# Sixteen decay columns computed with the first head's values, and decays by one product with three row parts

## The chip, the cores and the metric

The kernel runs on one core of one Trainium2 chip. The metric is the device time of one execution in microseconds; the median of several runs is taken. In what follows PE is TensorE (the matrix engine), ACT is ScalarE, DVE is VectorE, POOL is GpSimd and SP is SyncE, whose queue issues the transfers. Lines (L286) are those of the kernel before unless it says otherwise.

## The reference, cut to what matters

A trunk of two layers on a sequence of 1024 tokens with 1024 features, float32. Layer 0 is a softmax attention with a forgetting gate, layer 1 a gated linear attention (GLA); each is followed by a SwiGLU channel mixer, and every sub-layer is normalised and modulated by a conditioning vector. The change lies in the start of the GLA:

```
proj = h @ w_in                                    # 1024 x (512 + 512 + 1024 + 1024 + 16)
q, k, v, r, a_lr = split(proj, [512, 1024, 2048, 3072])
log_alpha = log_sigmoid(a_lr @ w_a2 + b_a) / 16    # a_lr: 1024 x 16, w_a2: 16 x 512
# per head (4 heads, 128 key and 256 value channels), in chunks of 64 tokens:
b = cumsum(log_alpha within the chunk)
q_in, k_in = q * exp(b), k * exp(-b);  k_dec = k * exp(b_last - b)
A = tril(q_in @ k_in.T);  o = A @ v + q_in @ state
state = exp(b_last) * state + k_dec.T @ v
o = rms_norm(o) * g_o * silu(r)
```

So the decays of every head come from 16 columns of the projection (a_lr, columns 3072 to 3087 of w_in), multiplied by a 16 x 512 matrix.

## The kernel before

**Numbers.** Every float32 operand of a product is split in two parts, hi (rounded to the format that PE reads fast) and lo (the rest), and a product is three matmuls, hi·hi, hi·lo and lo·hi, accumulated in PSUM: `mm3`, lines L286, L287 and L288. `split` makes the two parts: a cast on ACT (L174) and a subtraction on DVE (L175). Weights come by `load_w` (L209), which loads 8 k-tiles of 128 rows by 128 columns, or 4 by 256, into one of three raw buffers, casts them in two pieces on ACT (L223) and subtracts in four pieces, three on POOL and one on DVE (L227). `Weights.next` keeps three loads ahead of their use, in the order of one list. The hi and lo parts take turns through a ring of slots, so a later load's cast waits until the matmuls that read that slot are done.

**The start of the GLA.** `h1`, the normalised input, has features on partitions and tokens along the free axis, in eight tiles of hi and lo, and is made in two token halves of 512. With it the kernel computes, for head 0:

- the values, `gv_body`: per pair of token tiles (128 tokens each) one PSUM bank with 2 x 256 columns; `proj_tok` does 24 matmuls of 256 columns per token tile (8 k-tiles, three products). Two weight loads hold k-tiles 0 to 3 (`wv_0`) and 4 to 7 (`wv_4`).
- the 16 low-rank columns, `a_body`: weights `aw` from `load_w16` in a tile padded to 128 columns, with the hi part in columns 0 to 15, the lo part in 32 to 47 and zeros elsewhere; per token half 16 matmuls of 512 columns (`aps`, L1860 and L1861). `sum16` adds the two row groups; the result is split into `aT`, hi in rows 0 to 15 and lo in rows 32 to 47, tokens along the free axis.
- the decays, `gate_z`: per head and token half two matmuls of 512 columns (`z`, L1889 and L1890), of `aT` with the hi and with the lo part of `w2t`, the second matrix in two row copies; then absolute value on ACT (L1891) and minimum on DVE (L1892).
- `gate_body`: exponential and logarithm on ACT (L1899, L1900, each with a load of a function table), subtraction, prefix scan on DVE (L1901, L1904), `dec` (L1908), and the exponentials `ei` and `t2` (L1914, L1915).
- `head_front`: the keys `gk` and queries `gqp`, each two token halves of 24 matmuls of 512 columns, multiplied by the exponentials on DVE (L1929, L1930, L1944).
- `r_proj`: the output gates `gr`, four products of 24 matmuls of 512 columns (two value halves dv, two token halves hf), with SiLU on ACT (L2042).
- `head_back`: transposes of the decayed keys (`kdt`), the products within a chunk (`at`), the states (`kv`, `S_t`), the outputs (`go`), their norm and transposes (`ogt`). `weave` mixes into it what is left of `r_proj`; the values and decays of the next head follow in the program and are drawn in where the order allows.

**Order.** The engines' instruction orders come from a list scheduler that simulates the program when it is built, bound by data dependencies, by the order in which buffers of a ring are given out, and by manual orderings (`tc.issue_after`, `behind_all`). On the chip each engine then runs its list in order. In the PSUM the rings are: `pj` with three banks (gv, aps, z, gr, gk, gqp in turn), `opr` with two (go), and one each for `at`, `kv` and `trr` (transposes).

Before, the program text for head 0 reads: values of token tiles 0 to 3; low-rank columns and decays of half 0; gates `gr` (dv 0, hf 0); values of tiles 4 and 5; low-rank columns and decays of half 1 with `gate_body`; values of tiles 6 and 7; then `head_front` and `head_back`, into which the other three gate products go. A stream of conditioning products for later sub-layers (`ada1`: transfers `ad_s` on SP, L414; pieces on DVE, L475 and L477) is spread over the whole stage.

Of the kernel before, what the change touches and what calls it, by code (L numbers as in the profile page):

```python
# [9 lines left out]
F32 = mybir.dt.float32  # L10
FR = mybir.dt.float32r
# [5 lines left out]
P = 128  # L17
# [3 lines left out]
HALF = 512  # L21
# [32 lines left out]
def trunk(ctx, tc, x, c, ada_w, ada_b, norm1_g, norm2_g, ffn_w_in, ffn_w_out,  # L54
          fox_w_in, fox_b_f, fox_w_out, gla_w_in, gla_w_a2, gla_b_a, gla_g_o,
          gla_w_out, final_g, out, dbg=None, stop=None):
    nc = tc.nc
# [3 lines left out]
    big = ctx.enter_context(tc.tile_pool(name="big", bufs=1))  # L61
    psp = ctx.enter_context(tc.tile_pool(name="psp", bufs=1, space=bass.MemoryType.PSUM))
# [95 lines left out]
    ident = cst.tile([P, P], F32, name="ident")  # L158
# [14 lines left out]
    def split(hi, lo, src):  # L173
        nc.scalar.copy(hi, src)  # L174
        nc.vector.tensor_sub(lo, src, hi.bitcast(F32))  # L175

    wr = Ring(big, names[0:3])
    ws = Ring(big, names[3:9])
# [21 lines left out]
    def leave_ffn():  # L200
        if opr_:
            ws.q = deque(opr_["sg"] + list(opr_["r"].q))
            opr_.clear()

    def load_w(src, name, ws=ws, later=False):

        kk, m = src.shape[0] // P, src.shape[1]
        raw = wr([P, kk, m], F32, name)
        nc.sync.dma_start(raw, src.rearrange("(k p) m -> p k m", p=P))  # L209
        leave_ffn()  # L210
        w = Pair(ws([P, kk, m], FR, name + "h"), ws([P, kk, m], FR, name + "l"))
        flat = lambda t: t.rearrange("p k m -> p (k m)")
        hi, lo, rw = flat(w.hi), flat(w.lo), flat(raw)
        n = kk * m

        def behind(e):
            return tc.issue_after(split_after[e]) if split_after else ExitStack()

        def parts(his=(0, 1), los=(0, 1, 2, 3)):
            for i in his:  # L220
                cs = slice(i * n // 2, (i + 1) * n // 2)
                with behind("A"):
                    nc.scalar.copy(hi[:, cs], rw[:, cs])  # L223
            for i in los:
                cs = slice(i * n // 4, (i + 1) * n // 4)
                with behind("G" if i < 3 else "D"):
                    (nc.gpsimd if i < 3 else nc.vector).tensor_sub(lo[:, cs], rw[:, cs], hi[:, cs].bitcast(F32))  # L227
        if later:
            return w, parts
        parts()  # L230
        return w


    split_after = {}
# [31 lines left out]
    def sum16(out, t, ps):  # L266

        nc.scalar.copy(t, ps[32:48, :])
        nc.vector.tensor_add(out, ps[0:16, :], t)

    class Weights:
# [7 lines left out]
        def next(self):  # L279
            while self.loads and len(self.got) < self.depth:  # L280
                f, *a = self.loads.popleft()
                self.got.append(f(*a))
            return self.got.popleft()

    def mm3(ps, ah, al, bh, bl, start, stop):
        nc.tensor.matmul(ps, ah, bh, start=start, stop=False)  # L286
        nc.tensor.matmul(ps, ah, bl, start=False, stop=False)  # L287
        nc.tensor.matmul(ps, al, bh, start=False, stop=stop)  # L288
# [8 lines left out]
    def proj_tok(ps, w2, hs, t):  # L297

        ts_ = psl(t)
        for k in range(8):  # L300
            w = w2[k // 4]
            mm3(ps, hs[k].hi[:, ts_], hs[k].lo[:, ts_], w.hi[:, k % 4, :], w.lo[:, k % 4, :], k == 0, k == 7)
            yield 0.33


    acc_sl, s1_sl = names[9:10], names[10:11]
# [67 lines left out]
    for t in range(6):  # L374
        nt, src = (4, rows2[0:8, :]) if t < 4 else (2, crow)
# [32 lines left out]
    def last_of(e):  # L408
        return next(i for i in reversed(nc.cur_bb.bb.instructions) if i.engine == ENG[e])
# [95 lines left out]
    ada0, ada0p, ada1 = Pace(), Pace(), Pace()  # L505
# [169 lines left out]
    sp_ins, rb_ins, root_ins = [], [], {}  # L675
# [95 lines left out]
    sr, tr, orr, pj = ps_rings(2, 3, 1, 2)  # L771
# [169 lines left out]
    Wg = gla_w_in[0]  # L941
    loads = []
# [4 lines left out]
        loads += w_loads(W, D + (p + 1) * P)  # L947
    loads += out_loads(fox_w_out[0], 0, 4) + 2 * out_loads(fox_w_out[0], 4, 4)
    loads += ffn_loads(0)
    loads += v_loads(Wg, 1024) + [(load_w16, Wg[:, 3072:3088], "aw", ws, "all")]  # L950
    for h in range(4):
        if h:
            loads += v_loads(Wg, 1024 + h * 256)
# [5 lines left out]
    feed = Weights(loads)  # L959
# [119 lines left out]
    for n, (d, hf) in enumerate(rest0):  # L1079
# [23 lines left out]
        if n in late_tr:  # L1103
            tp, i = late_tr[n]
# [682 lines left out]
    rest_of_norm, norm_end = [], []  # L1787
# [20 lines left out]
    h1 = hs1  # L1808
# [10 lines left out]
    vr = Ring(big, take(5))  # L1819
    aslot, wslot = take(2)  # L1820
# [4 lines left out]
    kdr = Ring(big, take(2))  # L1825
# [11 lines left out]
    pj, atr, kvr, opr, trr = ps_rings(3, 1, 1, 2, 1)  # L1837
# [3 lines left out]
    on_t = big.tile([P, 2, 2, 256], F32, tag=on_slot, name="on_t")  # L1841
    QS = 128 ** -0.5

    w2raw = wr([64, 512], F32, "w2raw")
    nc.sync.dma_start(w2raw[0:16, :], gla_w_a2[0])
    nc.sync.dma_start(w2raw[32:48, :], gla_w_a2[0])
    w2t = big.tile([P, 2, 512], FR, tag=wslot, name="w2t")
    aT = big.tile([P, S], FR, tag=aslot, name="aT")

    def w2_split():  # L1850
        nc.gpsimd.memset(w2t.bitcast(F32), 0.0)
        nc.gpsimd.memset(aT.bitcast(F32), 0.0)
        for r0 in (0, 32):
            split(w2t[r0:r0 + 16, 0, :], w2t[r0:r0 + 16, 1, :], w2raw[r0:r0 + 16, :])

    def a_body(aw, hf, bt):
        ps = pj([P, HALF], F32, f"aps{hf}")
        cs = hsl(hf)
        for k in range(8):
            nc.tensor.matmul(ps, aw[:, k, :], h1[k].hi[:, cs], start=k == 0, stop=False)  # L1860
            nc.tensor.matmul(ps, aw[:, k, :], h1[k].lo[:, cs], start=False, stop=k == 7)  # L1861
        a = bt[1][0:16, cs]
        sum16(a, bt[0][0:16, cs], ps)
        nc.scalar.copy(aT[0:16, cs], a)
        nc.vector.tensor_sub(aT[32:48, cs], a, aT[0:16, cs].bitcast(F32))

    def gv_body(h, wv, tp, behind=None):

        ps = pj([P, 2, 256], F32, f"gv{h}{tp}")
        for i in range(2):  # L1870
            with tc.issue_after(behind) if behind is not None and i else ExitStack():
                run(proj_tok(ps[:, i, :], wv, h1, 2 * tp + i))
        if h:
            ada1(5.1)
        v = vr([P, 2, 2, 256], FR, f"gvt{h}{tp}")
        split(v[:, 0], v[:, 1], ps)
        return v

    def gate_tiles(h):
        return Tr([P, S], F32, f"b16_{h}"), Tr([P, S], F32, f"t2_{h}")  # L1880

    def gate_z(h, halves, bt=None):

        b16, t2 = bt or gate_tiles(h)
        hs_ = psl(h)
        for hf in halves:
            cs = hsl(hf)
            ps = pj([P, HALF], F32, f"z{h}{hf}")
            nc.tensor.matmul(ps, w2t[:, 0, hs_], aT[:, cs], start=True, stop=False)  # L1889
            nc.tensor.matmul(ps, w2t[:, 1, hs_], aT[:, cs], start=False, stop=True)  # L1890
            nc.scalar.activation(t2[:, cs], ps, AF.Abs, bias=bacol(h))  # L1891
            nc.vector.tensor_scalar(b16[:, cs], ps, bacol(h), 0.0, op0=ALU.add, op1=ALU.min)  # L1892
        return b16, t2
# [149 lines left out]
            done.add((dv, hf))  # L2043
            yield 0.01

    wv = [feed.next(), feed.next()]
    at = split_after["A"]
    split_after["A"] = norm_end[0]
    aw, aw_split = feed.next()
    split_after["A"] = at  # L2050
    split_after["G"] = after_norm
    aw_split()
    with behind_all():
        w2_split()
    split_after.update(marks)
    vt = [gv_body(0, wv, 0)]
    with tc.issue_after(sp_ins[-1]):
        vt.append(gv_body(0, wv, 1, rb_ins[-1]))
    split_after.update((e, last_of(e)) for e in "AD")
    with behind_all():  # L2060
        for f in rest_of_norm:
            f()
    split_after.update(marks)
    with tc.issue_after(rb_ins[-1]):
        bt = gate_tiles(0)
        a_body(aw, 0, bt)
        gate_z(0, (0,), bt)
        gs = [gsr([P, S], F32, f"gs0{i}") for i in range(2)]
        done = set()
        rg = r_proj(0, gs, done)  # L2070
        while (0, 0) not in done:
            next(rg)
    vt.append(gv_body(0, wv, 2))
    a_body(aw, 1, bt)
    b16, t2, ei, dec = gate_body(0, gate_z(0, (1,), bt))
    vt.append(gv_body(0, wv, 3))
# [105 lines left out]
```

## Time and profile before

| | |
|---|---|
| median of 3 runs | 2393.48 us (2393.46 to 2394.89) |
| profiled execution: span | 2392.7 us, 0.8 us under the median; no other time of this execution is given |
| PE busy | 2367.3 us, 99% of the span, 12344 matmuls |
| DVE, ACT, POOL busy | 74%, 47%, 44% |
| mean granted PE clock | 0.997 |
| start of head 0's values to its first keys | 1294.5 to 1337.2 us |

A row of the timeline has start and duration in us, the engine, the line, the operation, the written and read tiles, their shape (partitions x elements) and the count; in brackets stands the idle time of the engine before it and what ended that. Matmuls overlap with their successor: the price of one is the distance to the next start, not the duration shown. A row of the windows has, for a stretch, the length, then busy time and number of instructions of PE, PE's weight loads, DVE, ACT and POOL, the granted PE clock as a share of full speed, the share of the transfer engines in use and what they moved in GB/s.

### The profile page before, as it was taken

To read this page: it belongs to the slowest core of one execution; us is meant where nothing else is said; L and a number is where in the kernel's file an instruction comes from. 1 tells how busy PE (TensorE), PEld (TensorE's weight loads), DVE (VectorE), ACT (ScalarE), POOL (GpSimd) and SP (SyncE) were. 2 spreads that over 40 slices of the span, in tenths; PEclk is the share of its full clock that TensorE was granted. 3 is DMA by queue.
4 is the path that set the end of the run, shared out by engine and by line. 5 is a ranking of instruction groups with operands and counts; after the bars stand their busy time and mean duration, and the time that the engine had idled before them with its cause. 6 is when DMAs were issued, how large, how long until landed. Compare 5 with 4: busy or idle time off the path is not lost.

```text
span 2392.7 us, 35859 instructions
## 1 busy us (share of the span) xinstructions
PE 2367.3 (99%) x12344; PEld 2017.8 (84%) x12344; DVE 1770.0 (74%) x2984; ACT 1127.9 (47%) x2164; POOL 1046.2 (44%) x974
## 2 busy tenths in 40 slices
PE   8999999999999999999999999999999999999998
PEld 7888888888888888888888888898888888888888
DVE  6577787876698788876798565655687878775787
ACT  6656565664443333345325545453343334345326
POOL 1334444533446666643264221222345666643262
PEclk9999999999999999999999999999999999999999
DMA  7423333342435545457655242334424544457664
GB/s 254 151 79 112 102 119 93 121 142 78 150 113 178 176 162 168 168 203 266 223 183 161 68 119 87 100 113 132 143 99 154 183 150 154 154 186 258 227 199 147
DMA packets 336286, 363.43 MB, mean 152 GB/s; under 512 B 24860, under 2 KB 277944, under 8 KB 336104
## 3 DMA queue, kind: packets, MB, share of 16 engines
q1 hardware_dynamic: 336104, 361.15, 46.2%
q8 instruction: 97, 1.59, 0.3%
q14 instruction: 85, 0.70, 0.1%
HBM read 268.19 MB, written 92.86 MB: 151 GB/s over the span
## 4 chain that ended last, share of the span: by engine, by line
PE 89%; DVE 3%; DMA 3%; ACT 2%; issue 1%; SPq 1%; POOL 0%; DVEq 0%; POOLq 0%; ACTq 0%
PE p_b L288 16%; PE p_b L286 16%; PE p_b L287 16%; PE o_b L1211 2%; PE t_b L1197 2%; PE qk_b L286 2%; PE qk_b L287 2%; PE qk_b L288 2%; PE vps_b L288 1%; PE vps_b L286 1%; PE vps_b L287 1%; PE gr_b L286 1%; PE gr_b L287 1%; PE gr_b L288 1%; PE s_b L1165 1%; PE s_b L1166 1%
## 5 line engine op out<-in xcount | busy, mean ns | idle before, releaser
L175 DVE TENSOR_TENSOR o_s<-xv_s,o_s 128x512 fp32r<-128x512 f32 (+1 forms) x376 | 324.4, 868 | 62.8 <-ACT o_s L174 62.4
L174 ACT CAST o_s<-xv_s 128x512 fp32r<-128x512 f32 (+1 forms) x376 | 216.1, 587 | 293.9 <-PE p_b L288 242.3
L287 PE MATMUL p_b<-B,o_s 128*128 128x512 f32 x608 | 237.5, 391 | 0.0
L288 PE MATMUL p_b<-B,o_s 128*128 128x512 f32 x608 | 236.9, 390 | 0.0
L286 PE MATMUL p_b<-B,o_s 128*128 128x512 f32 x608 | 235.6, 391 | 0.0
L876 POOL TENSOR_TENSOR ex_s<-xv_s,xv_s 128x512 f32<-128x512 f32 (+1 forms) x64 | 86.8, 1357 | 288.0 <-DMA xv_s<-in_ffn_w_in_dram 118.2
L1177 POOL TENSOR_SCALAR lp_s<-lp_s,st 128x128 f32<-128x128 f32 (+7 forms) x128 | 97.5, 765 | 248.9 <-DVE st L1176 227.2
L286 PE MATMUL p_b<-T,o_s 128*128 128x512 f32 x480 | 186.7, 389 | 0.0
L287 PE MATMUL p_b<-T,o_s 128*128 128x512 f32 x480 | 186.7, 389 | 0.0
L288 PE MATMUL p_b<-T,o_s 128*128 128x512 f32 x480 | 181.2, 389 | 0.0
L288 PEld LDWEIGHTS p_b<-B,o_s 128*128 128x128 f32 x608 | 114.5, 188 | 23.8
L286 PEld LDWEIGHTS p_b<-B,o_s 128*128 128x128 f32 x608 | 114.6, 188 | 23.8
L287 PEld LDWEIGHTS p_b<-B,o_s 128*128 128x128 f32 x608 | 114.5, 188 | 23.8
L1175 ACT ACTIVATE lp_s<-lp_s,st 128x128 f32<-128x128 f32 (+7 forms) x128 | 99.3, 777 | 61.9 <-DVE st L1171 60.0
L878 POOL TENSOR_TENSOR xv_s<-ex_s,xv_s 128x512 f32<-128x512 f32 (+1 forms) x64 | 87.6, 1368 | 60.8 <-DVE o_s L175 58.2
L174 ACT CAST pt_s<-t_b 128x512 fp32r<-128x512 f32 (+1 forms) x160 | 79.8, 547 | 72.0 <-PE t_b L1197 71.4
L1559 DVE TENSOR_TENSOR ex_s<-ex_s,p_b 128x512 f32<-128x512 f32 x140 | 93.6, 680 | 25.1 <-PE p_b L288 24.9
L227 POOL TENSOR_TENSOR w_l_s<-w__s,w_h_s 128x256 fp32r<-128x256 f32 x90 | 69.3, 798 | 91.1 <-ACT w_h_s L223 51.9
L175 DVE TENSOR_TENSOR pt_s<-t_b,pt_s 128x512 fp32r<-128x512 f32 (+1 forms) x160 | 96.3, 630 | 15.7 <-ACT pt_s L174 15.2
L287 PEld LDWEIGHTS p_b<-T,o_s 128*128 128x128 f32 x480 | 90.1, 188 | 18.7
L286 PEld LDWEIGHTS p_b<-T,o_s 128*128 128x128 f32 x480 | 90.1, 188 | 18.7
L288 PEld LDWEIGHTS p_b<-T,o_s 128*128 128x128 f32 x480 | 90.1, 188 | 18.6
(1956 smaller groups left out, 7427.6 us busy)
## 6 DMA issues: line engine op xcount, KB each, us to landing
xv_s<-in_ffn_w_in_dram SPq DMA_DIRECT2D x176, 256.0 KB, 3.4
hid_B<-x SPq DMA_DIRECT2D x70, 512.0 KB, 2.9
ad_s<-in_ada_w_dram SPq DMA_DIRECT2D x384, 64.0 KB, 2.4
hid_T<-x SPq DMA_DIRECT2D x36, 512.0 KB, 2.9
xv_s<-in_ffn_w_out_dram SPq DMA_DIRECT2D x96, 192.0 KB, 5.0
ada_s<-in_ada_w_dram SPq DMA_DIRECT2D x96, 128.0 KB, 2.9
xv_s<-in_ffn_w_out_dram SPq DMA_DIRECT2D x40, 256.0 KB, 2.9
T2o<-hid_T SPq DMA_DIRECT2D x18, 512.0 KB, 8.8
```

Source lines behind the costliest of these rows:

```text
L174: nc.scalar.copy(hi, src)
L175: nc.vector.tensor_sub(lo, src, hi.bitcast(F32))
L227: (nc.gpsimd if i < 3 else nc.vector).tensor_sub(lo[:, cs], rw[:, cs], hi[:, cs].bitcast(F32))
L286: nc.tensor.matmul(ps, ah, bh, start=start, stop=False)
L287: nc.tensor.matmul(ps, ah, bl, start=False, stop=False)
L288: nc.tensor.matmul(ps, al, bh, start=False, stop=stop)
L876: nc.gpsimd.tensor_add(s1, a21, a22)
L878: nc.gpsimd.tensor_sub(a11, s1, a11)
L1175: nc.scalar.activation(lp, lp, AF.Exp, bias=mcur, scale=-1.0, accum_out=st[:, qi, 2:3])
L1177: nc.gpsimd.tensor_scalar(lp, lp, st[:, qi, 3:4], 1.0, op0=ALU.mult, op1=ALU.mult)
L1197: nc.tensor.transpose(tp[:, i, :], lps[qi][:, psl(2 * b + jj)], ident)
L1559: nc.vector.tensor_add(d, d if src is None else dest(G, src), ps)
```

## The change

1. `load_w` takes several sources for one tile. Head 0's values come with the 16 low-rank columns at their side, in three loads of 3, 3 and 2 k-tiles with 256 + 16 columns (`va_parts`); the load `aw` and `load_w16`'s use for it go.
2. `gv_first` replaces `gv_body` for head 0: each of the eight token tiles has a PSUM bank of its own (a ring `gvr` over the three banks of `pj` and the two of `opr`) and 24 matmuls of 272 columns. ACT copies the last 16 columns into `aS`; the 256 others are split as before, one token tile at a time.
3. `a_body` is now four transposes per token half, from `aS` (tokens on partitions) into a tile of 16 x 512 (`low_tr`). `aT` has three row parts: hi in 0 to 15, lo in 32 to 47, hi again in 64 to 79; `w2t` is one copy with rows hi, hi, lo at the same places. So one matmul per head and half gives the three products, in place of two matmuls.
4. In the program text the order is: values of tiles 0 to 3; gates (dv 0, hf 0); low-rank rows and decays of half 0; values of tiles 4 to 7; gates (dv 0, hf 1), which were in `head_back` before; low-rank rows and decays of half 1.

```diff
     def load_w(src, name, ws=ws, later=False):
-        kk, m = src.shape[0] // P, src.shape[1]
+        srcs = src if isinstance(src, tuple) else (src,)
+        kk, m = srcs[0].shape[0] // P, sum(s_.shape[1] for s_ in srcs)
         raw = wr([P, kk, m], F32, name)
-        nc.sync.dma_start(raw, src.rearrange("(k p) m -> p k m", p=P))
+        c0 = 0
+        for s_ in srcs:
+            nc.sync.dma_start(raw[:, :, c0:c0 + s_.shape[1]], s_.rearrange("(k p) m -> p k m", p=P))
+            c0 += s_.shape[1]
...
+    def va_parts(wmat, lo, ca):
+        return [((wmat[psl(k0, n), lo:lo + 256], wmat[psl(k0, n), ca:ca + 16]), f"wv{lo}_{k0}")
+                for k0, n in ((0, 3), (3, 3), (6, 2))]
+
+    def low_tr(ps, src, hf):
+        for i in range(4):
+            nc.tensor.transpose(ps[:, psl(i)], src[:, 4 * hf + i], ident)
...
-    loads += v_loads(Wg, 1024) + [(load_w16, Wg[:, 3072:3088], "aw", ws, "all")]
+    loads += [(load_w, *a) for a in va_parts(Wg, 1024, 3072)]
...
-    w2raw = wr([64, 512], F32, "w2raw")
-    nc.sync.dma_start(w2raw[0:16, :], gla_w_a2[0])
-    nc.sync.dma_start(w2raw[32:48, :], gla_w_a2[0])
-    w2t = big.tile([P, 2, 512], FR, tag=wslot, name="w2t")
+    w2raw = wr([P, 512], F32, "w2raw")
+    for r0 in (0, 32, 64):
+        nc.sync.dma_start(w2raw[r0:r0 + 16, :], gla_w_a2[0])
+    w2t = big.tile([P, 512], FR, tag=wslot, name="w2t")
...
-        for r0 in (0, 32):
-            split(w2t[r0:r0 + 16, 0, :], w2t[r0:r0 + 16, 1, :], w2raw[r0:r0 + 16, :])
-
-    def a_body(aw, hf, bt):
-        ps = pj([P, HALF], F32, f"aps{hf}")
+        for r0 in (0, 32, 64):
+            nc.scalar.copy(w2t[r0:r0 + 16], w2raw[r0:r0 + 16, :])
+        nc.vector.tensor_sub(w2t[64:80], w2raw[64:80, :], w2t[64:80].bitcast(F32))
+
+    def a_body(hf):
+        ps = trr([16, HALF], F32, f"aps{hf}")
         cs = hsl(hf)
-        for k in range(8):
-            nc.tensor.matmul(ps, aw[:, k, :], h1[k].hi[:, cs], start=k == 0, stop=False)
-            nc.tensor.matmul(ps, aw[:, k, :], h1[k].lo[:, cs], start=False, stop=k == 7)
-        a = bt[1][0:16, cs]
-        sum16(a, bt[0][0:16, cs], ps)
-        nc.scalar.copy(aT[0:16, cs], a)
-        nc.vector.tensor_sub(aT[32:48, cs], a, aT[0:16, cs].bitcast(F32))
+        low_tr(ps, aS, hf)
+        nc.scalar.copy(aT[0:16, cs], ps)
+        nc.vector.tensor_sub(aT[32:48, cs], ps, aT[0:16, cs].bitcast(F32))
+        nc.scalar.copy(aT[64:80, cs], ps)
+
+    def gv_first(t, wv, behind=None):
+        if t % 2 == 0:
+            vt.append(vr([P, 2, 2, 256], FR, f"gvt0{t}"))
+        ps = gvr([P, 272], F32, f"gv0{t}")
+        with tc.issue_after(behind) if behind is not None else ExitStack():
+            run(proj_tok(ps, wv, h1, t))
+        nc.scalar.copy(aS[:, t], ps[:, 256:272])
+        v = vt[-1]
+        split(v[:, 0, t % 2], v[:, 1, t % 2], ps[:, 0:256])
...
-            nc.tensor.matmul(ps, w2t[:, 0, hs_], aT[:, cs], start=True, stop=False)
-            nc.tensor.matmul(ps, w2t[:, 1, hs_], aT[:, cs], start=False, stop=True)
+            nc.tensor.matmul(ps, w2t[:, hs_], aT[:, cs], start=True, stop=True)
...
-    vt = [gv_body(0, wv, 0)]
+    gvr = Ring(psp, list(pj.q) + list(opr.q))
+    aS = big.tile([P, 8, 16], F32, tag=kdr.q[0], name="aS")
+    vt = []
+    gv_first(0, wv)
+    gv_first(1, wv)
     with tc.issue_after(sp_ins[-1]):
-        vt.append(gv_body(0, wv, 1, rb_ins[-1]))
+        gv_first(2, wv)
+        gv_first(3, wv, rb_ins[-1])
...
     with tc.issue_after(rb_ins[-1]):
-        bt = gate_tiles(0)
-        a_body(aw, 0, bt)
-        gate_z(0, (0,), bt)
         gs = [gsr([P, S], F32, f"gs0{i}") for i in range(2)]
         done = set()
         rg = r_proj(0, gs, done)
         while (0, 0) not in done:
             next(rg)
-    vt.append(gv_body(0, wv, 2))
-    a_body(aw, 1, bt)
+        a_body(0)
+        bt = gate_z(0, (0,))
+    for t in range(4, 8):
+        gv_first(t, wv)
+    while (0, 1) not in done:
+        next(rg)
+    a_body(1)
     b16, t2, ei, dec = gate_body(0, gate_z(0, (1,), bt))
-    vt.append(gv_body(0, wv, 3))
```

More of the change, by code (lines that the diff above doesn't have):

```diff
@@ L299, in proj_tok @@
         ts_ = psl(t)
+        n = 4 if len(w2) == 2 else 3
         for k in range(8):
-            w = w2[k // 4]
-            mm3(ps, hs[k].hi[:, ts_], hs[k].lo[:, ts_], w.hi[:, k % 4, :], w.lo[:, k % 4, :], k == 0, k == 7)
+            w = w2[k // n]
+            mm3(ps, hs[k].hi[:, ts_], hs[k].lo[:, ts_], w.hi[:, k % n, :], w.lo[:, k % n, :], k == 0, k == 7)
             yield 0.33
+    def va_parts(wmat, lo, ca):
[4 more added lines that the diff above has]
+            nc.tensor.transpose(ps[:, psl(i)], src[:, 4 * hf + i], ident)
     acc_sl, s1_sl = names[9:10], names[10:11]
@@ L1852, in w2_split, with gv_body @@
         nc.gpsimd.memset(aT.bitcast(F32), 0.0)
-        for r0 in (0, 32):
-            split(w2t[r0:r0 + 16, 0, :], w2t[r0:r0 + 16, 1, :], w2raw[r0:r0 + 16, :])
-    def a_body(aw, hf, bt):
-        ps = pj([P, HALF], F32, f"aps{hf}")
-        cs = hsl(hf)
-        for k in range(8):
-            nc.tensor.matmul(ps, aw[:, k, :], h1[k].hi[:, cs], start=k == 0, stop=False)
-            nc.tensor.matmul(ps, aw[:, k, :], h1[k].lo[:, cs], start=False, stop=k == 7)
-        a = bt[1][0:16, cs]
-        sum16(a, bt[0][0:16, cs], ps)
-        nc.scalar.copy(aT[0:16, cs], a)
-        nc.vector.tensor_sub(aT[32:48, cs], a, aT[0:16, cs].bitcast(F32))
-    def gv_body(h, wv, tp, behind=None):
+        for r0 in (0, 32, 64):
[3 more added lines that the diff above has]
+        ps = trr([16, HALF], F32, f"aps{hf}")
+        cs = hsl(hf)
+        low_tr(ps, aS, hf)
[11 more added lines that the diff above has]
+        split(v[:, 0, t % 2], v[:, 1, t % 2], ps[:, 0:256])
+    def gv_body(h, wv, tp):
         ps = pj([P, 2, 256], F32, f"gv{h}{tp}")
         for i in range(2):
[L1871 to L1874, printed above, removed]
+            run(proj_tok(ps[:, i, :], wv, h1, 2 * tp + i))
+        ada1(5.1)
         v = vr([P, 2, 2, 256], FR, f"gvt{h}{tp}")
@@ L2044, in r_proj @@
             yield 0.01
[L2046 to L2050, printed above, removed]
+    wv = [feed.next() for _ in range(3)]
     split_after["G"] = after_norm
-    aw_split()
     with behind_all():
```

## The prediction

> **What bounds the kernel now.** I read the first page, the windows, TensorE's (PE's) timeline, and the waits. The page says that nearly all of the span is PE:
>
> ```profile
> span 2392.7 us, 35859 instructions
> PE 2367.3 (99%) x12344; PEld 2017.8 (84%) x12344; DVE 1770.0 (74%) x2984; ACT 1127.9 (47%) x2164; POOL 1046.2 (44%) x974
> PE 89%; DVE 3%; DMA 3%; ACT 2%; issue 1%; SPq 1%; POOL 0%; DVEq 0%; POOLq 0%; ACTq 0%
> ```
>
> PE is busy for 99% of the span and carries 89% of the chain that ended last. So a PE matmul removed here is worth its start-to-start spacing, unless PE then waits for what the matmul hid. The result of the profiled run gives no time beside its span; the span is 0.8 us under the median of 2393.48, and I carry that offset. About 0.2% (4.8 us) is what a measurement can tell from no change: faster means under 2388.7, slower over 2398.3.
>
> The stretch that changes, by windows (start:end, length, then busy time and count of PE, PEld, DVE, ACT, POOL, the granted clock, DMA share, GB/s):
>
> ```profile
> 1300.00:1302.00 2.00, 2.00 (x15) 2.00 (x16) 1.08 (x4) 1.62 (x4) 0.84 (x1) 0.80 0.69 226
> 1302.00:1304.00 2.00, 2.00 (x11) 2.00 (x11) 0.90 (x2) 0.00 (x0) 2.00 (x3) 0.50 0.47 124
> ...
> 1306.00:1312.00 6.00, 6.00 (x53) 6.00 (x52) 5.88 (x10) 4.55 (x9) 1.83 (x3) 1.00 0.87 190
> 1312.00:1316.00 4.00, 4.00 (x19) 3.18 (x19) 4.00 (x5) 4.00 (x7) 1.69 (x2) 1.00 0.00 0
> ...
> 1393.00:1396.00 3.00, 1.64 (x14) 1.43 (x13) 1.71 (x2) 1.91 (x5) 0.00 (x0) 1.00 0.33 93
> ```
>
> PE is full until 1316. ACT is full from 1312 to 1316, and there the change adds ACT work; at 1393 PE has a hole.
>
> **What is removed.** PE's timeline, around both low-rank projections:
>
> ```profile
> 1309.07 0.28 PE L286 MATMUL gv_b<-wv_0h_s,h1h 128*128 128x256 f32 x1
> ...
> 1311.95 0.40 PE L1860 MATMUL aps_b<-h1h,aw_s 128*128 128x512 f32 x1
> ...
> 1315.60 0.45 PE L286 MATMUL gr_b<-h1h,w_h_s 128*128 128x512 f32 x1
> ...
> 1327.33 0.40 PE L1860 MATMUL aps_b<-h1h,aw_s 128*128 128x512 f32 x1
> ...
> 1330.98 0.28 PE L286 MATMUL gv_b<-wv_0h_s,h1h 128*128 128x256 f32 x1
> ```
>
> Sixteen low-rank matmuls take 1315.60 − 1311.95 = 3.65 us, and again 1330.98 − 1327.33 = 3.65: 7.30 us, 0.228 each. One token tile of values, 24 matmuls of 256 columns, takes 1311.95 − 1309.07 = 2.88: 0.120 each. Of the decay products the second of each pair goes:
>
> ```profile
> 1322.56 0.40 PE L1889 MATMUL z_b<-aT,w2t 128*128 128x512 f32 x1
> 1322.79 0.40 PE L1890 MATMUL z_b<-aT,w2t 128*128 128x512 f32 x1
> 1323.03 0.28 PE L286 MATMUL gv_b<-wv_4h_s,h1h 128*128 128x256 f32 x1
> ```
>
> ```profile
> L1890 PE MATMUL z_b<-aT,w2t x8: 389/392/397, 1322.8 to 1553.7; 128*128 128x512 f32 x8
> ```
>
> Eight times 0.23 is 1.84 us, all on PE's path. Removed in all: 9.14 us.
>
> **What is added on PE.** The 8 x 24 = 192 value matmuls become 272 wide, a width that the trace does not show. The neighbours are 256 at 0.120 and 512 at 0.228, so 16 more columns cost between nothing and 0.108 each, 0 to 20.7 us in all. I take the slope between the two rows, 0.108 x 16/256 = 0.0068 each, as 256 is 16 columns away and 512 is 240: 1.30 us. Eight transposes come in as two groups of four. The nearest row is:
>
> ```profile
> 1358.97 0.60 PE L1956 MATMUL kdt_b<-ident,t_s 128*128 128x128 f32 x4
> ...
> 1359.63 0.40 PE L287 MATMUL gr_b<-h1l,w_h_s 128*128 128x512 f32 x1
> ```
>
> Between them lies one 512-wide matmul, so four transposes cost 1359.63 − 1358.97 − 0.23 = 0.43; twice that is 0.86. PE work alone: −9.14 + 1.30 + 0.86 = **−6.98 us**.
>
> **What moves, and the new waits.** In the changed kernel as built, PE goes from the last values to aps of the second half, gk's first half (gk_0), gr of value half 0, second token half (gr_1; before, it filled head 0's back), z of the second half, gk_1, gqp_0, gqp_1. The pj ring has three banks, so gk_1 takes the bank that SiLU (ACT) empties of gr_1, and gqp_1 takes the bank that DVE empties of gk_0, which needs head 0's whole gate chain. Before, these had their banks free. The rows that price it:
>
> ```profile
> 1320.90 0.39 PE L288 MATMUL gr_b<-h1h,w_l_s 128*128 128x512 f32 x1
> ...
> 1321.33 0.60 ACT L2042 ACTIVATE gs_s<-gr_b 128x512 f32<-128x512 f32 x1 [3.30 <-PE gr_b L288]
> ...
> 1335.37 1.14 ACT L223 CAST w_h_s<-w__s 128x512 fp32r<-128x512 f32 x2 [2.25 <-PE gv_b L287]
> ...
> 1337.16 0.69 ACT L1891 ACTIVATE t_s<-z_b,vec 128x512 f32<-128x512 f32 x1 [0.65 <-PE z_b L1890]
> ...
> 1339.38 1.28 ACT L1899 ACT_TABLE_LOAD   x1
> ```
>
> ```profile
> 1345.28 0.48 DVE L477 SCALAR_TENSOR_TENSOR ad_s<-ad_s,c 128x256 f32<-128x256 f32 x1
> ...
> 1347.93 0.46 DVE L477 SCALAR_TENSOR_TENSOR ad_s<-ad_s,c 128x256 f32<-128x256 f32 x1
> ...
> 1351.40 0.68 DVE L1930 TENSOR_TENSOR t_s<-gk_b,t_s 128x512 f32<-128x512 f32 x1
> ```
>
> Call t0 the start of gr_1's last matmul. On ACT the cast of head 1's first value weights stands ahead of that SiLU; it writes the slot that gr_1 reads, so it cannot start before t0 + 0.2 (the second-last matmul, at t0 − 0.23, lasts about 0.4), and ends near t0 + 1.3 (1.14 by the cast row). SiLU then ends at t0 + 1.9. gk_1 would have started at t0 + 0.46, after the z matmul: a wait of 1.4 us. The absolute value follows (0.69), so the first table load is at about t0 + 2.5. In before, from that load (1339.38) to the end of L1930 (1352.08) are 12.7 us; two DVE pieces of the adaLN stream that stand inside this stretch (the two rows) are not there in the built order, which I value at 0.3 each: 12.1. gk_0's bank is free at t0 + 14.6. gk_1 and gqp_0, 48 matmuls of 0.228, run from t0 + 1.9 to t0 + 12.85. So gqp_1 waits 1.7. New waits: **+3.1 us**. Bounds: nothing, if the scheduler's picture of the overlap is the real one, to 4 us with the two DVE pieces still in the chain.
>
> **Old waits that should go.** In the whole recurrence around head 0 PE waited three times:
>
> ```profile
> 1394.60 0.39 PE L286 MATMUL go_b<-S_t,gq01h_s 128*128 128x256 f32 x1 [1.36 <-ACT S_t L174]
> ...
> 1401.35 0.30 PE L1992 MATMUL ogt_b<-ident,on_t 128*128 128x128 f32 x1 [0.25 <-DVE on_t L2030]
> ...
> 1402.85 0.39 PE L286 MATMUL go_b<-gvt_s,ahl_s 128*128 128x256 f32 x1 [0.96 <-ACT junk L2026]
> ```
>
> They sum to 2.57. All stand behind head 1's gate chain on ACT and DVE, which ran amid head 0's last states. In the built order head 1's z stands two state steps earlier (ahead of the third state, before it was ahead of the fifth), and its value matmuls spread between the states. I take 0.4 to be left, **−2.2 us**, by a walk through that order; bounds: all gone (−2.6), or all kept and more (the first rival).
>
> **What I cost at nothing.** The aw load, its memset and its splits go: they are off PE's path. The 16-column DMAs, the third row part of w2 and of aT, and narrower splits come in:
>
> ```profile
> ad_s<-in_ada_w_dram SPq DMA_DIRECT2D x72, 64.0 KB, 2.4
> ...
> wv_s<-in_gla_w_in_dram SPq DMA_DIRECT2D x4, 512.0 KB, 4.0
> ...
> aw_s<-in_gla_w_in_dram SPq DMA_DIRECT2D x1, 64.0 KB, 2.4
> ```
>
> ```profile
> 1286.28 0.38 SPq L251 DMA_DIRECT2D aw_s<-in_gla_w_in_dram  x1
> ...
> 1298.14 2.74 PE L745 MATMUL sp_b<-ones,se_s 128*128 128x1 f32 x24
> ...
> 1300.19 0.29 ACT L174 CAST aw_s<-aw_s 128x128 fp32r<-128x128 f32 x1
> ```
>
> The aw transfer is the same 16 columns of the same matrix: 2.4 us to landing. The last part of the weights is issued where aw was, 14 us before PE is done with the one-column matmuls ahead of its first use. On ACT four of the eight 16-column copies (at most 0.29 each, the price of 128 columns) and two more value casts fall into 1306 to 1316, where only 1.45 us of 6 and then none is free; the norm's second half ends some 1 to 2 us later, but PE does gr_0 (5.5 us) in front of most of the values that need it. If that cover fails, it costs up to 1 us, which is in the range.
>
> SP's queue: head 1's second value weights now stand behind 16 adaLN loads. The price of one is here, and the cast that waits for them:
>
> ```profile
> 1340.54 5.23 SPq L414 DMA_DIRECT2D ad_s<-in_ada_w_dram  x8
> ...
> 1353.30 1.13 ACT L223 CAST wv_4h_s<-wv_s 128x512 fp32r<-128x512 f32 x2
> ```
>
> On PE the first four tokens end at 1311.95 + 96 x 0.0068 = 1312.6; 11 values and 4 transposes bring 1314.4, gr_0 1319.9, the other 85 values and a z 1330.9, transposes and gk_0 1336.8, gr_1 1342.3, so t0 is near 1342. The last eight adaLN loads wait for DVE's use of their buffers, which by its built order stands behind the aT of the second half: near 1339, an estimate. At 5.23 for eight, the weights go out near 1344.2 and land, with some 0.5 to issue and 4.0, near 1348.7. Its cast stands on ACT just ahead of the decay exponentials, and PE's gqp_1 waits behind those. Its cast may start as late as t0 + 9.9 = 1352, just in time for the exponentials: 3.3 us to spare, after which it costs one for one.
>
> [...] The clock: at 1302 to 1304 it is 0.50, behind a run of 24 one-column matmuls; 11 matmuls take 2.00 where 0.120 each gives 1.32, and with the part in the window before, at 0.80, about 1 us was lost. But the window 1393:1396 holds the 1.36 us wait and shows 1.00. So I charge the new waits, 1.4 and 1.7 with 11 us of work between, with no slow clock; were each to bring one, it is +2 us, 2389.4. [...]
>
> **Sum.** −6.98 + 3.1 − 2.2 = −6.1; 2393.48 − 6.1 = **2387.4 us** (span 2386.6).
>
> **Rivals.**
> *The waits of head 0's back stay.* gr_1, 24 x 0.228 = 5.5 us of matmuls that wait for nothing, has left that back, so its waits lose cover. For: ACT and DVE have not less to do there. Against: head 1's values fill in. With the old 2.57 kept, −6.98 + 3.1 gives 2389.6; with all 5.5 of cover missing, 2395.1. Chance 0.27, all within 0.2%.
> *No new wait.* The gate chain is quicker, or banks free up: −6.98 − 2.2, 2384.3. Chance 0.13.
> *Slower: 272 columns are priced like 512.* Place: the 192 value matmuls. Each would cost 0.108 more, 20.7 in all in place of 1.30: 2406.8. It decides from +0.038 each (6.1 + 1.3 over 192), and is over 0.2% from +0.064. For: no row between 256 and 512. Against: the trace's two widths differ by nearly the ratio of the columns. Chance 0.06, with 0.02 for the late load of weights (over 14 us late).
> *The change doesn't do what it says*, or the saved work was hidden: 2393.5, no change. The built order has the wide matmuls, one z matmul in place of each pair and none of the low-rank ones, and PE is full; chance 0.02.
> My forecast's own case, 2385.5 to 2388.7, has 0.50.
>
> **Numbers.** Faster: 0.50 + 0.13 = 0.63. Same: 0.27 + 0.02 = 0.29. Slower: 0.08. The range 2383.8 to 2392.0 takes in the case without new waits, the forecast, and the lower half of the first rival; left out are its upper half and the slower cases, near 0.2.
>
> **What would show it.** In the profile after: gv rows at 0.127 spacing between 1306 and 1312; no aps rows of 512 columns but four 128-column ones per half; a PE wait of some 1.4 at the first gk row of the second half, put down to ACT, and of some 1.7 at the second gqp, put down to DVE; no or short waits at go in head 0. Wrong would be a gv spacing over 0.15, waits at go of over 3 us, or the cast of the second value weights starting with a DMA wait after 1352.

## The result, and the profile after

| | before | after |
|---|---|---|
| median of 21 runs | 2394.89 us (2393.33 to 2398.56) | 2390.13 us (2386.50 to 2395.76) |
| ratio | | 0.9981, 95% interval 0.9974 to 0.9987 |
| profiled execution: time, span | —, 2392.7 us | 2393.87, 2392.2 us |

The change makes the kernel faster by 0.19%, 4.5 us (3.1 to 6.2). That is just short of the 0.2% from which the prediction speaks of faster. The forecast was 6.1 us, 2387.4 in a range of 2383.8 to 2392.0. The execution of the changed kernel that was profiled took 3.7 us more than its median. The page of the changed kernel:

```profile
span 2392.2 us, 35827 instructions
PE 2362.3 (99%) x12312; PEld 2012.5 (84%) x12312; DVE 1770.5 (74%) x2985; ACT 1128.8 (47%) x2178; POOL 1046.5 (44%) x976
PE 82%; DVE 8%; DMA 4%; ACT 2%; issue 2%; POOL 1%; SPq 1%; DVEq 0%; POOLq 0%; ACTq 0%
```

Thirty-two matmuls are gone (40 out, 8 transposes in). The chain that ended last now runs through DVE for 8% of the span, before 3%, but that is no price: 70 of the 100 us that DVE gained in it lie between 1100 and 1300, nearly all of it ahead of the changed stage, where PE waited 0.7 us in all. What counts are the waits of PE, here of the changed kernel from 1290 to 1420 (us in total, times, longest):

```profile
PE gqp_b L290 <- DVE t_s L1949: 2.9, 1, 2.9
PE gk_b L290 <- ACT gs_s L2061: 1.3, 1, 1.3
PE go_b L292 <- DVE ahl_s L175: 0.2, 1, 0.2
```

Before, this window had the three waits in head 0's back, 2.57 us. They are gone, one of 0.25 for another reason has come (the third row, at 1395.15), and the two that the prediction named stand in front, at gk and at gqp.

PE's timeline of the changed kernel has the prices of what was added (lines are those of the changed kernel, L290 to L292 for the three products):

```profile
1311.65 0.29 PE L290 MATMUL gv_b<-wv_0h_s,h1h 128*128 128x272 f32 x1
...
1314.67 0.29 PE L290 MATMUL gv_b<-wv_0h_s,h1h 128*128 128x272 f32 x1
1314.79 0.29 PE L291 MATMUL gv_b<-wv_0l_s,h1h 128*128 128x272 f32 x1
1314.92 0.49 PE L316 MATMUL aps_b<-ident,aS 128*16 128x128 f32 x3
1315.16 0.37 PE L292 MATMUL gv_b<-wv_0h_s,h1l 128*128 128x272 f32 x1
1315.37 0.29 PE L290 MATMUL gv_b<-wv_0h_s,h1h 128*128 128x272 f32 x1
```

One token tile of 24 matmuls takes 1314.67 − 1311.65 = 3.02 us, 0.126 each; before it took 2.88. The eight tiles cost 1.12 us more. Three transposes cost 1315.37 − 1314.79 − 2 x 0.126 = 0.33, and the fourth about 0.1.

Now the gate chain that both waits hang on: PE, ACT, DVE and POOL of the changed kernel in order of time.

```profile
1343.98 0.39 PE L292 MATMUL gr_b<-h1h,w_l_s 128*128 128x512 f32 x1
1344.20 0.39 PE L1909 MATMUL z_b<-aT,w2t 128*128 128x512 f32 x1
1345.91 0.50 PE L290 MATMUL gk_b<-h1h,w_h_s 128*128 128x512 f32 x1 [1.31 <-ACT gs_s L2061]
...
1359.96 0.50 PE L290 MATMUL gqp_b<-h1h,w_h_s 128*128 128x512 f32 x1 [2.88 <-DVE t_s L1949]
```

```profile
1344.22 1.14 ACT L227 CAST wv_0h_s<-wv_s 128x512 fp32r<-128x512 f32 x2 [4.29 <-PE gr_b L291]
1345.27 0.59 ACT L2061 ACTIVATE gs_s<-gr_b 128x512 f32<-128x512 f32 x1
...
1346.45 1.28 ACT L1918 ACT_TABLE_LOAD   x1
```

```profile
1352.47 3.27 DVE L1923 TENSOR_TENSOR_SCAN b_s<-ad_s,t_s 128x512 f32<-128x512 f32 x2
1355.77 0.52 DVE L1927 TENSOR_SCALAR dec<-b_s 128x8 f32<-128x8 f32 x1
...
1359.22 0.68 DVE L1949 TENSOR_TENSOR t_s<-gk_b,t_s 128x512 f32<-128x512 f32 x1
```

```profile
1352.19 4.07 POOL L231 TENSOR_TENSOR wv_4l_s<-wv_s,wv_4h_s 128x256 fp32r<-128x256 f32 x3 [4.98 <-ACT wv_4h_s L227]
```

The last matmul of gr starts at t0 = 1343.98. The cast of head 1's weights holds the SiLU back (1344.22, after 4.29 us of waiting for gr's reads), gk starts when the SiLU is done, and gqp when DVE has emptied gk's first bank at 1359.90, t0 + 15.9. In that chain the two scans take 3.27 us and the small dec 0.52, both of them while POOL works from 1352.19 to 1356.26.

Behind the second wait the clock falls. Windows of the changed kernel (columns as in the prediction):

```profile
1350.00:1360.00 10.00, 7.12 (x33) 5.57 (x31) 6.78 (x9) 7.26 (x19) 4.07 (x3) 1.00 0.56 148
1360.00:1370.00 10.00, 10.00 (x39) 8.07 (x40) 8.16 (x15) 8.82 (x23) 2.13 (x3) 0.83 0.18 46
1370.00:1380.00 10.00, 10.00 (x57) 8.66 (x56) 7.07 (x14) 3.90 (x6) 0.62 (x1) 1.00 0.39 112
```

A mean of 0.83 over 10 us is 1.7 us of full speed lost, 3.4 us at half.

**The account of the profiled executions.** The stage is counted from head 0's first value matmul to the first transpose of head 1's keys, here before and after:

```profile
1294.50 0.28 PE L286 MATMUL gv_b<-wv_0h_s,h1h 128*128 128x256 f32 x1
...
1438.97 0.60 PE L1956 MATMUL kdt_b<-ident,t_s 128*128 128x128 f32 x4
```

```profile
1296.28 0.28 PE L290 MATMUL gv_b<-wv_0h_s,h1h 128*128 128x272 f32 x1
...
1438.09 0.60 PE L1975 MATMUL kdt_b<-ident,t_s 128*128 128x128 f32 x4
```

That is 1438.97 − 1294.50 = 144.47 us before and 1438.09 − 1296.28 = 141.81 after: −2.66. Up to there the work is −7.30 − 0.92 (four of the eight z matmuls) + 1.12 + 0.86 = −6.24; the new waits are +4.19, the old ones −2.57 + 0.25, the slow clock +1.7: −2.7 in all, as measured.

Outside the stage the two profiles differ too. The stage began 1.78 us later after the change (1296.28 against 1294.50; PE's clock over the first 60 us was 0.86 there and 1.00 before), and what follows it took 0.38 us more, so the two spans differ by 0.5 us only. Of the 3.7 us above the median the slow clock behind the wait can therefore be 1.7 at most. In the ten profiles of this case the stage begins anywhere between 1292.5 and 1298.6 us, so the total of a single execution says little about a change of a few us; the stage length and the medians say more.

### The profile page after: what moved, and what is told of

It is laid out like the page before. It is cut to its first block, busy times and chain, and to the rows that moved or that the text cites. A ratio compares the mean times of both kernels' runs of the same rounds, so it can differ in the third digit from the quotient of the medians.

```text
span 2392.2 us, 35827 instructions
## 1 busy us (share of the span) xinstructions
PE 2362.3 (99%) x12312; PEld 2012.5 (84%) x12312; DVE 1770.5 (74%) x2985; ACT 1128.8 (47%) x2178; POOL 1046.5 (44%) x976
## 4 chain that ended last, share of the span: by engine, by line
PE 82%; DVE 8%; DMA 4%; ACT 2%; issue 2%; POOL 1%; SPq 1%; DVEq 0%; POOLq 0%; ACTq 0%
PE p_b L290 15%; PE p_b L292 15%; PE p_b L291 15%; PE o_b L1224 2%; PE t_b L1210 2%; PE qk_b L290 1%; PE qk_b L291 1%; PE qk_b L292 1%; PE gr_b L290 1%; PE gr_b L291 1%; PE vps_b L292 1%; PE vps_b L290 1%; PE vps_b L291 1%; PE gr_b L292 1%; PE s_b L1178 1%
## 5 line engine op out<-in xcount | busy, mean ns | idle before, releaser
L292 PE MATMUL p_b<-B,o_s 128*128 128x512 f32 x608 | 237.2, 391 | 0.0
L290 PE MATMUL p_b<-B,o_s 128*128 128x512 f32 x608 | 236.0, 391 | 0.0
L290 PE MATMUL p_b<-T,o_s 128*128 128x512 f32 x480 | 186.7, 389 | 0.0
L292 PE MATMUL p_b<-T,o_s 128*128 128x512 f32 x480 | 181.2, 389 | 0.0
L292 PEld LDWEIGHTS p_b<-B,o_s 128*128 128x128 f32 x608 | 114.7, 189 | 24.0
L290 PEld LDWEIGHTS p_b<-B,o_s 128*128 128x128 f32 x608 | 114.7, 189 | 23.9
L175 DVE TENSOR_TENSOR pt_s<-t_b,pt_s 128x512 fp32r<-128x512 f32 (+1 forms) x160 | 96.3, 630 | 15.9 <-ACT pt_s L174 15.4
L290 PEld LDWEIGHTS p_b<-T,o_s 128*128 128x128 f32 x480 | 90.1, 188 | 18.8
L292 PEld LDWEIGHTS p_b<-T,o_s 128*128 128x128 f32 x480 | 90.1, 188 | 18.6
```

## The experiments

The stage length in what follows is measured between the same two instructions, each in the run's own profile. Medians and ratios are against the kernel before on the same chip. The kernel before had a median of 2394.89 us in the result's comparison, 2394.46 in those of the first four experiments and 2393.67 in those of the last four, so a distance between two versions is given by medians and, where it matters, by ratios; where the intervals of two ratios overlap, the distance is not clear of the noise.

**The place of z.** The decay product of half 1 ahead of the gate product:

```diff
-    while (0, 1) not in done:
-        next(rg)
     a_body(1)
-    b16, t2, ei, dec = gate_body(0, gate_z(0, (1,), bt))
+    zt_ = gate_z(0, (1,), bt)
+    with tc.issue_after(last_of("P")):
+        while (0, 1) not in done:
+            next(rg)
+    b16, t2, ei, dec = gate_body(0, zt_)
```

> The change, with one order turned: the decay product of the second half is made to stand ahead of the gate product gr (value half 0, second half) instead of behind it; everything else is the change's. Theory (the new waits come from the place of gr: it delays the start of head 0's gate chain, and gqp_1 waits for that chain's end): after z now stand 72 matmuls of 0.227 us (16.4 us) ahead of gqp_1 instead of 48, the chain takes 13 to 16 us, so the waits of 1.3 us at gk and 2.9 us at gqp go, and with them the slow clock behind the long wait. Total 3 to 6 us less than the change, 7 to 10 less than the kernel before. Rival (head 0's back keeps costing what the fronts save: the time is lost to latency of head 0 as a whole): the waits show up again at at, kv or go, the sum stays near 5 us, and the time is within 1 us of the change.

2386.89 us, ratio 0.9972 (0.9963 to 0.9981). Its waits up to head 1's keys:

```profile
PE z_b L1909 <- ACT aT L1876: 1.1, 1, 1.1
PE kdt_b L1975 <- DVE kdl_s L175: 0.8, 1, 0.8
PE kv_b L290 <- DVE Sf L2001: 0.4, 1, 0.4
PE at_b L291 <- DVE gq00l_s L175: 0.2, 1, 0.2
PE go_b L290 <- ACT S_t L174: 0.2, 1, 0.2
```

The waits at gk and gqp are gone, as expected; a part comes back, 1.1 at z itself, which now stands too close behind aT, and 1.6 spread over the back. The time is 3.2 us under the change's median and 2.2 by the ratios, at the lower end of what the theory expected or just under it, against under 1 by the rival; as the two intervals overlap, the totals alone don't decide between them. The rival has a share of truth: of the change's 4.4 us of waits, 2.7 are waited here at other places.

**The banks.** Head 0's gk and gqp from the ring of five, the three banks turned by one behind them:

```diff
-            ps = pj([P, HALF], F32, f"gk{h}{hf}")
+            ps = (pj if h else gvr)([P, HALF], F32, f"gk{h}{hf}")
...
-            ps = pj([P, HALF], F32, f"gqp{h}{hf}")
+            ps = (pj if h else gvr)([P, HALF], F32, f"gqp{h}{hf}")
...
     b16, t2, ei, dec = gate_body(0, gate_z(0, (1,), bt))
+    pj.q.rotate(-1)
```

> The change, with head 0's gk and gqp written into the ring of five PSUM banks (gvr) instead of three, and the order of the three banks turned by one behind them; the scheduler also swaps some matmuls of gqp. Theory (the waits are for a bank): no wait at gk or gqp in head 0, although z and gr keep their order; 3 to 5 us less than the change if nothing else is late, but the products at need the gate chain some 21 us after z, so a new wait of up to 1 us may show there. Rival (not the bank, but the chain itself is what head 0 waits for): the 4.2 us of waits move to the transposes of the decayed keys or to at, and the time is that of the change.

2385.88 us, ratio 0.9960 (0.9948 to 0.9973). Up to head 1's keys one wait is left:

```profile
PE kdt_b L1975 <- DVE kdl_s L175: 0.6, 1, 0.6
```

The gate chain is no faster here (the scans take 3.26 us), z and gr stand as in the change, and yet the waits are gone: they were for a bank, and the rest of head 0 had room for the chain's length. The stage takes 135.87 us in its profile, 8.6 under the kernel before; −6.24 of work, −2.57 of old waits and 0.63 give 8.2.

**The move alone.** In the kernel before, gr (dv 0, half 1) ahead of the second low-rank product:

```diff
     vt.append(gv_body(0, wv, 2))
+    while (0, 1) not in done:
+        next(rg)
     a_body(aw, 1, bt)
```

> The kernel before, with one edit of the change: the gate product gr (value half 0, second half) is pulled out of head 0's back to stand ahead of the second half's low-rank product; the 16 columns stay a product of their own. Theory (the place of z decides, not the move as such): here the built order has 24 gr, 16 aps, 46 values and then z, with 74 matmuls (16.6 us) between z and gqp_1, so no wait arises at gk or gqp; head 1's values fill head 0's back, and the time is within 2 us of the kernel before. Rival (the first rival of the prediction: gr is missing as cover in head 0's back): 2 to 5 us slower, with more waits at go.

2395.53 us, ratio 1.0002 (0.9994 to 1.0011): no change. The waits, though, are not absent. In head 0's back they moved towards its middle:

```profile
PE kdt_b L1956 <- DVE kdl_s L175: 1.9, 1, 1.9
PE at_b L287 <- DVE gq00l_s L175: 0.6, 1, 0.6
PE kv_b L286 <- DVE Sf L1982: 0.5, 1, 0.5
...
PE go_b L286 <- ACT S_t L174: 0.4, 1, 0.4
PE gqp_b L286 <- DVE t_s L1930: 0.4, 1, 0.4
```

At gqp only 0.4 is waited, so far the theory holds. The cover that the prediction's first rival spoke of is missed too, at the transposes of the keys rather than at go. In the profile the stage takes 147.96 us, 3.5 more than before: 1.7 more of waits and 1.7 of slow clock behind the longest. By the median of the runs, the move alone gains and loses nothing that is clear of the noise.

**DVE and POOL.** The lo parts of head 1's value weights by DVE alone, all orders kept:

```diff
-                with behind("G" if i < 3 else "D"):
-                    (nc.gpsimd if i < 3 else nc.vector).tensor_sub(...)
+                g = i < 3 and not name.startswith("wv1280")
+                with behind("G" if g else "D"):
+                    (nc.gpsimd if g else nc.vector).tensor_sub(...)
```

> The change, with the lo parts of head 1's value weights made by DVE alone (four pieces) where POOL made three of the four; the orders of all engines are otherwise the change's. Theory (the scan of 2 x 1.6 us instead of 2 x 1.2 and the slow first dec are POOL's work beside DVE): the two scans take 2.4 us together and dec 0.16, and the wait at gqp falls from 2.9 to about 1.6 us, 1.3 us less than the change, and 1 to 1.5 more where the clock then stays up. Rival (the scan is slow for another reason, such as the transfers at that time): scans stay near 3.3 us and the wait near 2.9 us.

2388.10 us, ratio 0.9975 (0.9966 to 0.9984). DVE's timeline and PE's waits of this kernel:

```profile
1356.53 2.34 DVE L1924 TENSOR_TENSOR_SCAN b_s<-ad_s,t_s 128x512 f32<-128x512 f32 x2
1358.90 0.17 DVE L1928 TENSOR_SCALAR dec<-b_s 128x8 f32<-128x8 f32 x1
```

```profile
PE gqp_b L291 <- DVE t_s L1950: 1.6, 1, 1.6
PE gk_b L291 <- ACT gs_s L2062: 1.3, 1, 1.3
PE go_b L293 <- DVE ahl_s L175: 0.2, 1, 0.2
```

Scans, dec and the wait are where the theory put them; the rival falls. With POOL out of the way the wait is 1.6 against the 1.7 of the prediction. The clock stands at 1.00 in the windows behind it. The time is 2.0 us under the change by the medians and 1.4 by the ratios, whose intervals overlap; what POOL costs is shown by the trace and not by the total.

**The move undone.** The change without the move (the two lines `while (0, 1) not in done: next(rg)` left out):

> The change without its move: the gate product gr (value half 0, second half) is left to head 0's back as before; the 272-wide values, the transposes and the single decay products stay. In the built order z of the second half now stands behind both products gk instead of between gr and gk_1, so gqp_0 and gqp_1 come 0 and 24 matmuls behind z, and on ACT a cast of head 1's weights stands inside the gate chain. Theory (what PE waits for in front is set by the number of matmuls between z and gqp_1: 74 before, 48 in the change, here 24 or 5.5 us, against a chain of 13 to 16 us): gqp_0 waits 1 to 2 us for z's bank and gqp_1 some 7 us or more, 7 to 10 us in all against 4.2; head 0's back then has its cover and loses under 1 us. Time 2 to 6 us above the change, near the kernel before. Rival (moving gr is what costs the waits): without the move no wait at gqp, and 4 us less than the change.

2397.11 us, ratio 1.0017 (1.0008 to 1.0026), 7.0 us above the change by the medians and 8.6 by the ratios. Its waits in the stage:

```profile
PE gqp_b L290 <- DVE t_s L1949: 6.8, 1, 6.8
PE gqp_b L290 <- DVE b_s L1911: 1.6, 1, 1.6
PE go_b L290 <- ACT junk L2045: 0.9, 1, 0.9
PE go_b L290 <- ACT S_t L174: 0.8, 1, 0.8
```

8.4 us at gqp: the rival, by which moving gr costs the waits, is false. Gr between the transposes that prepare z and z itself is work that fits there; without it the built order puts z behind both gk, and gqp meets the chain with 24 matmuls as cover. The total came out 1 to 3 us above the expected band; the clock around and behind the 6.8 us wait (0.56 from 1350 to 1360, 0.93 to 1370) was not in it, and 1.75 us of the old waits at go stayed.

Beside the move alone this says more than either run does by itself: the move without the columns gains nothing (1.0002), the columns without the move are slower than the kernel before (1.0017), and only the two together are faster (0.9981).

**Both edits that helped.** Five banks and DVE alone:

> The two edits that helped, together: five banks for head 0's gk and gqp, and DVE alone for the lo parts of head 1's values. Theory: no wait is left at gk or gqp, so the quicker scan has nothing on PE's path to shorten but the 0.6 us wait at the second transposes of the keys; within 1 us of the five banks alone, 7 to 9.5 us less than the kernel before. Rival (the gate chain still sets head 0's end): the 1.2 us of the scan come on top, 10 us or more.

2386.09 us, ratio 0.9965 (0.9952 to 0.9977), no different from the banks alone (0.9960) within the noise. The wait at kdt is gone, but 0.8 at kv and 0.4 at go have come. So the scans' 0.9 us (2.34 here, 3.26 in the banks alone) found no place to show, as the theory had it, and either version, some 8 us under the kernel before, beats it and the change.

**A longer wait.** The DVE version with one more pass on ACT in head 0's chain, which adds nothing to the result:

```diff
+        if h == 0:
+            nc.scalar.activation(t2, t2, AF.Abs)
         nc.scalar.activation(t2, t2, AF.Exp, scale=-1.0)
```

> The change with DVE alone for the lo parts of head 1's values (whose wait at gqp was 1.6 us, with the clock at 1.00 behind it), and one more pass of absolute value over 128 x 1024 on ACT in head 0's gate chain, without effect on the result: it lengthens the wait by about 1.1 us, to 2.7. Theory (a wait of PE near 2 us or more halves the clock for one stretch of 3.4 us, which costs 1.7 us): the windows behind the wait show a clock that lacks 3.4 us of half speed, and the time is 2.5 to 3 us above the run without the extra pass. Rival (the low clock behind the change's wait of 2.9 us came from elsewhere, and a wait costs its length): clock 1.00 behind it, 1.1 us above.

2391.38 us, ratio 0.9989 (0.9981 to 0.9998), 3.3 us above the DVE version. PE waited 3.88 at gqp, 2.3 more, not 1.1: DVE's order had turned as well, with a weight subtraction at 1354.37 between the scans and dec, which came 1.3 us later for it, at 1355.69. Its windows:

```profile
1350.00:1360.00 10.00, 6.12 (x26) 4.81 (x25) 6.41 (x12) 7.24 (x19) 0.00 (x0) 0.96 0.39 100
1360.00:1370.00 10.00, 10.00 (x42) 8.10 (x42) 8.48 (x16) 8.38 (x21) 2.32 (x3) 0.87 0.18 52
```

They lack 0.4 and 1.3, 1.7 us again. So the clock did fall behind the longer wait in this profile, as the theory has it; since the wait grew by more than planned, the medians alone (3.3 against 2.3 + 1.7) don't settle the price.

**The cast behind.** On ACT, head 1's first weights behind the logarithm:

```diff
         nc.scalar.activation(t2, t2, AF.Ln, bias=1.0)
+        if h == 0:
+            split_after["A"] = last_of("A")
```

> The change, with the casts of head 1's first value weights (and of head 0's last gate weights) ordered behind the logarithm of head 0's gate chain on ACT, so that nothing stands ahead of the SiLU at gr's end. Theory (SiLU is late because the cast waits for the slot that gr reads): the wait at gk falls from 1.3 to 0.5 or 0.6 us, and the gate chain starts 1 us earlier against z. The wait at gqp gains only what the chain gains over gk, some 0.2, unless the casts' subtractions on POOL now slow the scan more. Rival (SiLU is late by its own distance to gr): 1.3 us stay.

2393.34 us, one run.

```profile
PE gqp_b L290 <- DVE t_s L1951: 6.3, 1, 6.3
PE go_b L292 <- DVE ahl_s L175: 0.6, 1, 0.6
PE gk_b L290 <- ACT gs_s L2063: 0.5, 1, 0.5
```

The wait at gk fell to 0.5, as expected: the cast ahead of SiLU was its cause. But POOL's subtractions now stand beside the scans, which take 3.37 us, and DVE's piece of them stands ahead of dec, which comes at 1355.09, and gqp waits 6.3. That is far beyond what the expectation allowed for; a weight load that is put out of the way of one step landed on the next.

## Why the prediction was right, and where it was off

- **Removed and added work**: −6.98 predicted, −7.16 by the rows after (1.12 for the width instead of 1.30, transposes 0.43 per four in both). The slope between the widths 256 and 512 was the right price for 272: 0.126 measured, 0.127 foretold. The rival of 272 priced like 512 is dead by the same row.
- **The wait at gk**: 1.4 predicted, 1.31 measured, with the cast at t0 + 0.24 and SiLU's end at t0 + 1.9. The cast behind shows its cause.
- **The wait at gqp**: 1.7 predicted, 2.88 measured. This is the term that was mis-sized. The chain was taken from the first table load to the end of L1930 in the trace before, less 0.6, 12.1 us; it measured 13.45 (1346.45 to 1359.90). The step left out is that the scans, which before ran with POOL idle and took 2.33, would now have POOL beside them, as the late weights are subtracted just then. Scans and dec became 1.3 us longer; the DVE version takes POOL away, and the wait is 1.6.
- **The old waits in head 0's back**: 0.4 predicted to be left, 0.25 measured. The first rival, that they stay because gr has left, is wrong for this order. In the move alone, where gr has left too, head 0's back has 3.5 us of waits at other places; in the move undone, where gr stayed, 1.75 of the old ones were left.
- **No slow clock behind the new waits**: wrong in the profiled execution. The prediction had priced it at about 1 us for each wait, 2389.4 for both; it came behind the longer wait alone, and cost 1.7. The 1 us was read from the windows up to 1304; the same stretch before went on to 1304.6, by a clock of 0.70 from 1304 to 1305, and lost 1.7 as well. The hole of 1.36 us at 1393, with the clock at 1.00, was not long enough to tell what one of 2.9 would bring.
- **The late load of head 1's weights** did no harm by its arrival: its cast began at 1351.49, t0 + 7.5, with t0 + 9.9 allowed. The harm came from its subtraction on POOL, as said above.

With the terms as measured the sum is −7.16 + 4.19 − 2.32 = −5.3 without the slow clock and −3.6 with it; the runs say −4.5, between the two. In how many executions the clock fell is not shown, as only one was profiled.

So the mechanism was right, and two terms of the sum were off: the wait at gqp was too short, and the clock behind it stood at nothing. The time lies in the stated range, but outside the forecast's own band of 2385.5 to 2388.7, and the gain of 0.19% just misses what the prediction called faster and gave 0.63. Of the 2.7 us between the forecast 2387.4 and 2390.13, 1.4 is the base, 2393.48 by three runs in the forecast and 2394.89 by 21 here. That the time lies near the first rival's 2389.6 is chance: the waits that this rival kept are gone.

## What to carry to other kernels

When work is taken out in front of a latency chain, count the matmuls that stand between the chain's start and the first one that needs its end, by the built order: here 74 (the move alone), 48 (the change) and 24 (the move undone) of 0.227 us met a chain of about 15 us and gave waits of 0.4, 2.9 and 6.8. Taking work out and filling its place belong together; here neither gained alone. Two banks more at that place were worth 4 to 5 us, about as much as the change itself, since they let PE run past the chain. And price a chain's vector steps with whatever will run on POOL beside them, not with what ran there before: the two scans took 2.33 us with POOL idle and 3.27 beside it.

## What the runs showed of the hardware

- **PE's clock fell to half behind waits of 1.84 to 3.88 us.** Behind waits of 1.36 (before) and 1.60 (DVE version) the granted clock was 1.00. Behind 2.88 (change) and 3.88 (longer wait) 1.7 us of full speed were missing, which is 3.4 us at half: in steps of 1 us from 1360 the change's clock is 0.84, 0.50, 0.50, 0.50 and 0.95. Far ahead of the stage 1.7 us were missing too, behind 2.07 us at 417.12 (before; 0.57, 0.50, 0.50 and 0.72 in steps of 1 us from 417) and behind 1.84 us at 417.86 (change; 0.84 from 417.8 to 419, then 0.50 to 422). Behind the 1.94 us at kdt in the move alone it was the same amount:

```profile
1360.00:1370.00 10.00, 9.37 (x51) 7.70 (x50) 8.61 (x13) 6.89 (x17) 4.43 (x6) 1.00 0.58 159
1370.00:1380.00 10.00, 8.06 (x36) 6.41 (x35) 6.97 (x15) 4.97 (x9) 0.00 (x0) 0.83 0.39 107
```

  The same stretch also follows the 24 one-column matmuls at the stage's start, and in two of the ten profiles (z first, DVE version) two of them do. These are the windows of the version with z first:

```profile
1300.00:1304.00 4.00, 4.00 (x23) 4.00 (x23) 1.52 (x6) 2.99 (x6) 2.27 (x3) 0.59 0.58 189
1304.00:1308.00 4.00, 4.00 (x21) 4.00 (x21) 0.00 (x0) 0.00 (x0) 2.65 (x5) 0.56 0.70 185
```

  There 0.41 x 4 + 0.44 x 4 = 3.4 us are lost, against 1.7 in the kernel before. Each of these cases is one profile; where between 1.60 and 1.84 us the limit lies, if there is one, and what sets the length of the stretch, stays open.
- **POOL slows DVE's scans.** Two scans of 128 x 512 took 2.33 or 2.34 us with POOL idle (before, DVE version, banks and DVE, longer wait, move undone) and 3.26 to 3.37 with POOL subtracting (change, z first, five banks, cast behind); POOL's three pieces took 4.07 beside them, against 2.29 earlier in the change, when DVE was busy for about half of that time. For the scans that is 40% more (3.26 against 2.33). The first small dec took 0.52 beside POOL (change) and 0.17 without it (DVE version). By what POOL holds DVE up is not shown.
- **The format of the hi and lo parts.** Products of the parts cost 0.228 us at 512 columns and 0.120 at 256, 0.45 and 0.47 ns a column; a float32 transpose of 128 columns cost 0.11 (0.43 for four), 0.84 ns a column. But a product of the parts with 128 columns (at, 12 of them from 1360.79 to 1362.08 in the kernel before) cost 0.11 as well, and 128 is the one width at which these rows compare the two, so what the format gains is not shown by them.
